# The first down-projection of a two-FFN transformer layer, rewritten as seven block products for latents and context together

## The chip, the cores and the metric

One core of one Trainium2 chip runs the whole layer as a single program. The metric is device time in microseconds (us), shorter being better. Three executions of the kernel before took 2646.32, 2648.31 and 2648.55 us, median 2648.31. A further execution was profiled and took 2648.12 us; its trace covers 2646.3 us from the first to the last instruction.

## What is computed

The layer takes 1024 latent tokens and 256 context tokens, each 1024 wide. It runs a SwiGLU feed-forward block (FFN 1), an attention stage that reads latents and context, and a second SwiGLU block (FFN 2) on the latents alone. Only FFN 1 and the modulation around it matter here:

```python
def _swiglu(h, w1, w3, w2):
    return (jax.nn.silu(h @ w1) * (h @ w3)) @ w2
...
m  = jnp.split((jax.nn.silu(c) @ w_ada[l] + b_ada[l])[:, None, :], N_MOD, axis=-1)
mc = jnp.split(jax.nn.silu(c_ctx) @ w_ada[l] + b_ada[l], N_MOD, axis=-1)
x     = _residual(x, _swiglu(_modnorm(x, g[0], m[0], m[1]), ffn1_w1[l], ffn1_w3[l], ffn1_w2[l]), g[1], m[2], HALF_STEP)
h_ctx = _residual(h_ctx, _swiglu(_modnorm(h_ctx, g[0], mc[0], mc[1]), ffn1_w1[l], ffn1_w3[l], ffn1_w2[l]), g[1], mc[2], HALF_STEP)
```

The widths are 1024 in, 2816 in the middle (22 blocks of 128), 1024 out. Everything is float32.

## The kernel before, in words

**Precision.** Every float32 operand is split into a high and a low part: ScalarE (ACT) rounds the value into the high part, VectorE (DVE) subtracts to get the low part (`split_to`, L197). A product is then three TensorE (PE) matmuls, high by high, high by low and low by high (`mm3`, L158). Every matrix that PE reads therefore costs one ACT instruction and one DVE instruction per 512 columns before it can be used.

**Order.** A stage is a `Plan` (L163): a list of main steps, each a piece of PE work, and side steps (loads, splits, sums) hung on step numbers with `spread`. The program is written out in that order, and with `pinned` set every engine executes its instructions exactly in it. Engines do not wait for a step number; they run ahead until an instruction needs something that isn't there. `store` (L134) puts a transfer to DRAM two steps later than the data is made. All transfers go through one queue, SP's.

**Stages around the change.** First comes the latents' up-projection, computed as seven block products instead of eight (Winograd's variant of Strassen's scheme; `Unit`, L458): first `plan_leads`, then `plan_rest` (L600), where the last 22 units are finished. Each latent result (silu(w1) times w3, in DRAM tensor `gd`) is stored. Then follows the down-projection. Its 22 blocks of the middle width are taken in ten groups, nine of two and one of four (`gs`, L1089). In each group every one of ten token tiles (0 to 7 latent, 8 and 9 context; 128 tokens each) does two halves of 512 output columns (`Down.tile`, L897). The result of a group is added to the sum in SBUF by DVE.

The context's up-projection is folded into these groups: 44 blocks (`ctx_up`, L1107), each 24 matmuls with 256 columns, stand between the tiles of the first nine groups (L1140). Their weights (512 KB a block) are loaded and split by side steps, and so are two parts of the modulation (`ada_steps((4, 3))`, L1168). A third part, `ada_steps((2,))`, runs beside the latents' up-projection (L1084).

In the last group the tiles finish one after the other in the order 8, 9, 0 to 7. Behind each runs a chain (`residual_steps`, L639, placed by `plan_chains`, L665): ACT squares and sums the row, POOL takes the inverse root, DVE scales and adds the residual in two instructions, ACT and POOL do the same once more, and ACT writes the normalised tile.

**The stage behind.** The projections (`punits`, L1235) use tokens 0 to 511 first: `fill0` turns tiles 0 to 3 into operand planes, and `plan_leads` then does pairs of units, each with two pieces of 12 matmuls, a first product into a PSUM bank of the pool `m` (three banks) and a second one added into the same bank. `fill1` does the same for tiles 4 to 7 while the leads run. `Unit.split` has to prepare the first four weight pieces before the leads begin (L1248).

**A model in the same kernel.** The second FFN's down-projection is already done in seven block products (`Down7`, L752): 7 products of 11 steps, each step four token tiles with three matmuls of 512 columns each, going round four PSUM banks. Its inputs are the quarter matrices (`Quarters`, L672) and the weights' differences (`WeightQuarters`, L712), which are formed during the up-projection's `plan_rest` and pass through DRAM.

Of the kernel before, what the change touches and what calls it, by code (L numbers as in the profile page):

```python
# [9 lines left out]
F32R = mybir.dt.float32r  # L10
# [5 lines left out]
P = 128  # L16
# [27 lines left out]
def hybrid_block(ctx: ExitStack, tc: tile.TileContext, a: dict, out: bass.AP):  # L44
# [234 lines left out]
    class AdaSum(Ada):  # L279


        def __init__(self, m):
            self.m = m
            self.acc = [[T2() for _ in range(2)] for _ in range(2 if m < 5 else 1)]
# [14 lines left out]
        def end(self, v, h):  # L299

            pb, s = PB("v"), ST(4)
# [7 lines left out]
    def ada_steps(ms):  # L309
# [4 lines left out]
        def step(m, k, h):  # L314
            if m not in cur:
                cur[m] = AdaSum(m)
            if k:
                cur[m].step(k - 1, h)
            if k < KD:
                cur[m].load(k, h)  # L320

        def end(m, v, h, last):
            cur[m].end(v, h)
# [428 lines left out]
    class Down7:  # L752
# [22 lines left out]
        def product(self, i, t):  # L775
# [3 lines left out]
            mm3(self.banks[t], [x[:, t * P:(t + 1) * P] for x in a], w, k == 0 and o in (0, 2, 3), k == NP - 1)  # L779
            open_group[0] = False  # L780

# [56 lines left out]
    def up_units(h, w1, w3, gd, quarters=None):  # L838
# [3 lines left out]
        def pair_(p):  # L842
# [6 lines left out]
            def emit3(i, ci, x, bank):  # L849
                y = s.pop((i, ci))  # L850
                vec.tensor_tensor(y, x, y, op=ALU.mult)
                if quarters:
                    quarters.take(p, i, ci, y)
                else:
                    store(gd[2 * p + i, :, ci * 512:(ci + 1) * 512], y)
# [8 lines left out]
    lap = [0]  # L864

    def PD():
        lap[0] = (lap[0] + 1) % 8
        return PB("smvsmvsm"[lap[0]])

    class Down:  # L870


        def __init__(self, w2, gd, ys, fs):
            self.w2, self.gd, self.ys, self.fs = w2, gd, ys, fs
            self.w, self.g, self.c, self.r = {}, {}, {}, {}

        def loads(self, f, key="v"):
            self.r[f] = load(self.w2[f], key=key), load(self.gd[f], key=key)

        def steps(self, fs=None, key="v"):  # L880

            fs = fs or self.fs

            def one(f, e):
                self.w.setdefault(f, []).append(split(self.r[f][0][:, e * 512:(e + 1) * 512]))

            def two(f):
                self.g[f] = split2(self.r.pop(f)[1])

            s = []  # L890
            for f, after in zip(fs, fs[1:] + [None]):
                s += [lambda f=f: one(f, 0), lambda f=f: one(f, 1), lambda f=f: two(f)]
                if after is not None:
                    s[-2] = lambda f=f, n=after: (one(f, 1), self.loads(n, key))
            return s

        def tile(self, t, es=range(2)):  # L897
            ys, fs = self.ys, self.fs
            g = self.g if t < 8 else self.c
            c = slice((t % 8) * P, (t % 8 + 1) * P)  # L900
            if fs[0] == 0 and 0 in es:
                ys[t] = V()
            for e in es:
                o = slice(e * 512, (e + 1) * 512)
                pd = PD()
                for x, f in enumerate(fs):
                    mm3(pd, [y[:, c] for y in g[f]], self.w[f][e], x == 0, x == len(fs) - 1)
                if fs[0] == 0:
                    act.copy(ys[t][:, o], pd)
                else:  # L910
                    vec.tensor_tensor(ys[t][:, o], ys[t][:, o], pd, op=ALU.add)

    def groups(sizes):
        f, made = 0, []
        for n in sizes:
            made.append(list(range(f, f + n)))
            f += n
        return made
# [16 lines left out]
    gd = DR([NF, P, NLAT])  # L935
    units1 = up_units(h1, a["f1w1"], a["f1w3"], gd)
# [101 lines left out]
    def shift_led(p):  # L1038
# [4 lines left out]
        store(gd[2 * p, :, 0:512], x)  # L1043
# [39 lines left out]
    plan_rest(plan, units1)  # L1083
    plan.spread(ada_steps((2,)), rest1 + 10, len(plan.main) - 10)  # L1084
# [4 lines left out]
    gs = groups((2,) * 9 + (4,))  # L1089
    ys = {}  # L1090
    xc = []
    hc = [None]

# [4 lines left out]
    steps = []  # L1098
    cw, cr, cg, cc = {}, {}, {}, {}

    def ctx_load(f, x):
        cr[f, x] = load(a[("f1w1", "f1w3")[x]][f], key="v")

    def ctx_split(f, x, e):
        cw.setdefault((f, x), []).append(split(cr[f, x][:, e * 512:(e + 1) * 512]))

    def ctx_up(f, x):  # L1107
        o = PB("m")[:, :NCTX]
        for k in range(KD):
            hi, lo = cw[f, x][k // 4]  # L1110
            b = slice((k % 4) * P, (k % 4 + 1) * P)
            mm3(o, [hi[:, b], lo[:, b]], hc[0].get(k), k == 0, k == KD - 1)
        if x == 0:
            t = cg[f] = T2()
            act.activation(t[:, :NCTX], o, AF.Silu)
        else:
            g = cg.pop(f)[:, :NCTX]
            vec.tensor_tensor(g, g, o, op=ALU.mult)
            t = T2(F32R)
            cc[f] = split_to(t[:, :NCTX], t[:, NCTX:], g)  # L1120

    downs = [Down(a["f1w2"], gd, ys, fs) for fs in gs]
    for d in downs:
        d.c = cc
    o = len(plan.main)
    plan.spread([lambda: downs[0].loads(0, "u")], o - 9, o - 8)
    plan.spread(downs[0].steps(key="u"), o - 7, o)
    plan.spread(first_steps((8, 9), xc), o - 4, o - 2)
    ups = [(f, x) for f in range(NF) for x in range(2)]
    ctx_at = []  # L1130
    pos = {}
    for i, d in enumerate(downs):
        last = i == len(downs) - 1
        o = len(plan.main)
        if last:
            for t in [8, 9] + list(range(8)):
                pos[t] = len(plan.main) + 1
                plan.step(*[lambda d=d, t=t, e=e: d.tile(t, (e,)) for e in range(2)])
        else:
            order = ([None] * 4 + list(range(10)) if i == len(downs) - 2 else  # L1140
                     [0, 1, 2, 3, 4, None, 5, None, 6, None, 7, None, None, 8, 9])
            for t in order:
                if t is None:
                    f, x = ups.pop(0)
                    ctx_at.append((len(plan.main), f, x))
                    plan.step(lambda f=f, x=x: ctx_up(f, x))
                else:
                    plan.step(lambda d=d, t=t: d.tile(t))
        e = len(plan.main)
        if i == 0:  # L1150
            plan.spread([lambda: normal(xc[0]), lambda: normal(xc[1]), make_hc], o - 1, o)
            plan.spread([lambda k=k: steps[k]() for k in range(KD)], o + 1, o + 5)
        if i < len(downs) - 2:
            n = downs[i + 1]
            plan.spread([lambda n=n: n.loads(n.fs[0])], o, o + 1)
            plan.spread(n.steps(), o + 3, e)
        elif not last:
            n = downs[i + 1]
            plan.spread([lambda n=n: n.loads(n.fs[0])], o - 2, o - 1)
            plan.spread(n.steps(), o, e)  # L1160
# [1044 lines left out]
```

## Time and profile before

| | |
|---|---|
| median of three executions | 2648.31 us (2646.32 to 2648.55) |
| profiled execution, its time / its span | 2648.12 / 2646.3 us |
| granted TensorE clock, mean | 0.995 |
| DVE / ACT / POOL busy | 1861.2 (70%) / 1173.0 (44%) / 229.1 us (9%) |
| LDWEIGHTS (PEld) busy | 2222.1 us (84%), overlaps the matmuls |
| data moved | 460.57 MB, mean 174 GB/s |
| latents' up-projection, `plan_rest` | 139.82 to 462.68 us |
| down-projection with the context's up-projection | 462.68 to 905.91 us |
| first lead unit of the projections starts | 906.70 us |
| FFN 2: `plan_rest` / down-projection | 2083.15 to 2423.86 / from 2423.86 us |

How to read the lines below. A timeline row gives the start in us from the span's start, the duration, the engine, the line of the kernel, the operation, output from inputs by the names of their pools (`bm`, `bs`, `bv` are PSUM banks; `xu`, `xv`, `t` SBUF tiles), the shape, and how many alike were merged. In brackets stands idle time before it and what ended that. A matmul's own duration overlaps the next one's, so the pace of PE is the distance between starts. A row of the windows view gives, for a stretch of the span, its length, then busy time and instruction count of PE, PEld, DVE, ACT and POOL, the granted PE clock, the share of time that the DMA engines were busy and what they moved. The first row of a window whose edges cut a merged group counts only the part inside.

### The profile page before, as it was taken

How to read it: one execution, taken by the hardware profiler on the slowest of the kernel's cores; microseconds unless marked ns; L12 is line 12 of the kernel's file. 1: busy time of each engine (PE TensorE's matmuls, PEld its weight loads, DVE VectorE, ACT ScalarE, POOL GpSimd, SP SyncE). 2: the span in 40 equal slices, each digit the busy share in tenths (PEclk: the TensorE clock that was granted, in tenths of full speed). 3: DMA queues.
4: the chain of work that ended last, by engine and by line, in shares of the span. 5: the costliest groups of instructions: out<-in, count | busy, mean ns of one | idle time of the engine just before them, and what ended most of it. 6: DMA issues, size and time to landing. Idle time of an engine off the chain costs nothing.

```text
span 2646.3 us, 38182 instructions
## 1 busy us (share of the span) xinstructions
PE 2596.5 (98%) x13610; PEld 2222.1 (84%) x13610; DVE 1861.2 (70%) x3525; ACT 1173.0 (44%) x2248; POOL 229.1 (9%) x380
## 2 busy tenths in 40 slices
PE   7999999999999999999999999999999999999998
PEld 5888888888888788799888999998788888888887
DVE  4778876587876676666467988886625788778557
ACT  4532223532223763331346987774246322224533
POOL 0000000000000400000102432221011000000001
PEclk9999999999999999999999999999999999999999
DMA  7444433453433564477789942214325566546755
GB/s 285 159 154 152 147 116 123 139 176 109 173 110 104 210 220 156 163 258 231 218 287 276 252 116 75 75 30 171 112 80 172 190 237 224 187 170 251 271 187 195
DMA packets 220429, 460.57 MB, mean 174 GB/s; under 512 B 25488, under 2 KB 64592, under 8 KB 220240
## 3 DMA queue, kind: packets, MB, share of 16 engines
q1 hardware_dynamic: 220240, 458.14, 52.3%
q8 instruction: 107, 1.75, 0.3%
q14 instruction: 82, 0.67, 0.1%
HBM read 338.71 MB, written 119.34 MB: 173 GB/s over the span
## 4 chain that ended last, share of the span: by engine, by line
PE 68%; issue 18%; DVE 6%; ACT 5%; DMA 2%; POOL 1%; SPq 0%; DVEq 0%; POOLq 0%; ACTq 0%
PE bs L153 31%; PE bm L153 19%; PE bv L153 15%; PE bm L156 2%; ACT xu L1832 1%; DVE t L120 1%; DVE xv L120 1%; DVE xu L1699 1%; DVE xu L120 1%; DMA w<-d 1%; ACT t L1858 1%; DVE t L1859 1%; PE bs L156 1%; ACT t L120 1%; POOL st L120 1%
## 5 line engine op out<-in xcount | busy, mean ns | idle before, releaser
L153 PE MATMUL bm<-xu,xu 128*128 128x512 f32 (+1 forms) x2271 | 551.1, 387 | 1.4 <-DVE xu L120 1.1
L153 PEld LDWEIGHTS bm<-xu,xu 128*128 128x128 f32 x2271 | 417.9, 188 | 83.2 <-DVE xu L120 1.9
L153 PE MATMUL bs<-xu,xu 128*128 128x512 f32 (+1 forms) x1875 | 460.5, 385 | 0.5 <-DVE xu L120 0.4
L120 ACT CAST xu<-t 128x512 fp32r<-128x512 f32 x402 | 238.7, 618 | 392.4 <-DVE t L120 333.3
L153 PEld LDWEIGHTS bs<-xu,xu 128*128 128x128 f32 x1875 | 346.9, 188 | 67.7 <-DVE xu L120 0.8
L120 DVE TENSOR_TENSOR xu<-t,xu 128x512 fp32r<-128x512 f32 x402 | 265.9, 687 | 143.0 <-ACT xu L120 143.0
L153 PE MATMUL bs<-xv,xu 128*128 128x512 f32 (+1 forms) x1488 | 354.1, 387 | 5.1 <-DVE t L120 5.1
L153 PEld LDWEIGHTS bs<-xv,xu 128*128 128x128 f32 x1488 | 278.2, 189 | 62.3 <-issue 7.1
L153 PE MATMUL bv<-xv,xu 128*128 128x512 f32 x1276 | 318.6, 389 | 0.0
L153 PEld LDWEIGHTS bv<-xv,xu 128*128 128x128 f32 x1276 | 239.5, 188 | 49.7
L120 POOL TENSOR_SCALAR st<-st 128x1 f32<-128x1 f32 x72 | 38.0, 528 | 2061.2 <-ACT t L120 1999.7
L153 PE MATMUL bs<-w,w 96*128 96x512 f32 (+3 forms) x832 | 207.2, 368 | 7.7 <-DVE st L1724 7.1
L120 DVE TENSOR_TENSOR xu<-xu,xu 128x512 fp32r<-128x512 f32 (+2 forms) x219 | 149.3, 688 | 77.3 <-ACT xu L120 75.1
L153 PE MATMUL bm<-t,xu 128*128 128x256 f32 (+1 forms) x1272 | 166.0, 288 | 0.6 <-ACT t L120 0.4
L153 PEld LDWEIGHTS bm<-t,xu 128*128 128x128 f32 x1272 | 160.7, 191 | 5.6 <-ACT t L120 0.8
L120 DVE TENSOR_TENSOR xu<-xv,xu 128x512 fp32r<-128x512 f32 (+2 forms) x184 | 131.5, 739 | 47.3 <-ACT xu L120 44.1
L120 DVE TENSOR_TENSOR t<-t,t 128x512 f32<-128x512 f32 (+2 forms) x222 | 142.4, 643 | 25.8 <-ACT t L120 22.8
L153 PE MATMUL bv<-t,w 128*128 128x256 f32 x896 | 152.1, 290 | 3.7 <-ACT t L1858 1.7
L153 PEld LDWEIGHTS bv<-t,w 128*128 128x128 f32 x896 | 133.5, 191 | 19.4 <-DVE t L1859 5.0
L153 PE MATMUL bv<-xu,xu 128*128 128x512 f32 x530 | 142.7, 390 | 0.0
L120 ACT CAST xu<-xu 128x512 fp32r<-128x512 f32 (+2 forms) x211 | 127.7, 617 | 29.0 <-DMA xu<-in_wc 11.8
L153 PEld LDWEIGHTS bs<-w,w 96*128 96x128 f32 (+1 forms) x832 | 124.1, 191 | 17.0 <-DVE st L1724 10.1
(194 smaller groups left out, 3590.1 us busy)
## 6 DMA issues: line engine op xcount, KB each, us to landing
d<-t SPq DMA_DIRECT2D x321, 256.0 KB, 2.4
t<-d SPq DMA_DIRECT2D x204, 256.0 KB, 5.2
xu<-in_f1w SPq DMA_DIRECT2D x64, 512.0 KB, 3.9
xv<-in_f1w SPq DMA_DIRECT2D x64, 512.0 KB, 3.6
xu<-in_f2w SPq DMA_DIRECT2D x58, 512.0 KB, 4.5
t<-in_wada SPq DMA_DIRECT2D x112, 256.0 KB, 3.9
w<-d SPq DMA_DIRECT2D x112, 256.0 KB, 6.5
xv<-d SPq DMA_DIRECT2D x42, 512.0 KB, 5.6
```

What stands on the lines that cost most here:

```text
L120: return lambda *x, **y: pin(f(*x, **y))
L153: return pin(nc.tensor.matmul(o, s, m, start=start, stop=stop, skip_group_check=open_group[0]))
L156: return pin(nc.tensor.transpose(o, x, i))
L1699: nc.vector.tensor_scalar(dst, src, 1.0, FMIN, op0=ALU.mult, op1=ALU.max, accum_out=m)
L1832: nc.scalar.activation(x, x, AF.Exp, bias=n_[:, s:s + 1], accum_out=l[:, i:i + 1])
L1858: nc.scalar.copy(t[0], pb)
L1859: nc.vector.tensor_tensor(t[1], pb, f32(t[0]), op=ALU.subtract)
```

## The change

Three things change, all of them in FFN 1 and its surroundings.

The down-projection becomes seven block products over latents and context together. `Down7Context` inherits from `Down7`. A step now has five matmul groups of three (four latent tiles and one for the context) over five PSUM banks; per product the banks are listed in `BANKS`, and two products add into the banks of the one before. The context's tokens are cut into halves of 128, so one token tile stands for each quarter matrix. The last three of the 77 steps are done tile by tile (`tail`), which finishes latent tiles 4 to 7 and context tile 9; latent tiles 0 to 3 and context tile 8 are complete earlier.

The context's up-projection, all 44 blocks in a row, becomes a stage of its own between the latents' up-projection and the down-projection. Its results are turned into quarters (`ContextQuarters`), stored and loaded back as the latents' are. The latents' up-projection now also feeds `Quarters` and `WeightQuarters` as FFN 2 does.

The modulation parts move one stage later: `ada_steps((2,))` stands beside the context's up-projection, `(4,)` and `(3,)` beside the down-projection. The chains of tiles 0 to 3 and 8 start two steps apart, those of 4 to 7 and 9 one tail step apart; `fill0` ends three steps before the leads begin.

```diff
+    class Down7Context(Down7):
+        TAIL = 3
+        BANKS = ("mmmvv", None, "sssmm", "mvvss", "smmvv", "mmmvv", None)
...
+        def product(self, i, t):
+            if t < 4:
+                return super().product(i, t)
...
+            c = slice((k % 4) * P, (k % 4 + 1) * P)
+            mm3(self.banks[t], [x[:, c] for x in self.c[o, k // 4]], self.w[i][1], k == 0 and self.fresh(o), k == NP - 1)
...
+        def step(self, i):
+            o, k = i // NP, i % NP
+            if k == 0 and self.fresh(o):
+                self.banks = [PB(x) for x in self.BANKS[o]]
+            for t in range(5):
+                self.product(i, t)
+            if k == NP - 1:
+                for t in range(5):
+                    self.out(o, t)
...
-    plan_rest(plan, units1)
-    plan.spread(ada_steps((2,)), rest1 + 10, len(plan.main) - 10)
+    plan_rest(plan, units1, quarters1)
+    plan.spread(wq1.steps(), rest1, len(plan.main) - 8)
...
+    plan.spread([lambda t=t: xc.append(load(xin(t))) for t in (8, 9)], o - 9, o - 8)
+    plan.spread([lambda: normal(xc[0]), lambda: normal(xc[1]), make_hc], o - 7, o - 5)
+    plan.spread([lambda k=k: steps[k]() for k in range(KD)], o - 5, o - 1)
+    plan.step(*[lambda x=x: ctx_up(x) for x in range(2 * NF)])
+    for x in range(2 * NF):
+        plan.spread([lambda x=x: ctx_load(x)], o + x - 4, o + x - 3)
+        plan.spread([lambda x=x, e=e: ctx_split(x, e) for e in range(2)], o + x - 2, o + x)
+    plan_quarters(plan, quarters1, NP - 1, o)
+    plan.spread(ada_steps((2,), True), o + 1, len(plan.main) - 1)
+    down1 = Down7Context(quarters1, wq1, cq1, ys)
+    o, tail = down1.plan(plan)
...
+    plan.spread(ada_steps((4,), tag="s"), o + 2, o + 2 * NP)
+    plan.spread(ada_steps((3,), tag="s"), o + 2 * NP + 2, o + 5 * NP + 6)
+    pos = {t: o + 5 * NP + 1 + 2 * i for i, t in enumerate((0, 1, 2, 3, 8))}
+    pos.update({t: tail + i for i, t in enumerate((4, 5, 6, 7, 9))})
...
-    plan.spread([lambda k=k: fill0s()[k]() for k in range(KD)], pos[3] + 5, o + 1)
+    plan.spread([lambda k=k: fill0s()[k]() for k in range(KD)], pos[3] + 5, o - 3)
```

Two places in the order of instructions matter below. The first is ACT in the context's up-projection. Before, in the second half of the down-projection, these rows stand there; ACTIVATE is the silu of an even block, read from a PSUM bank, and CAST the high part of a split, 256 wide for a context result, 512 or 1024 wide for weights and latent results:

```order
L120 ACTIVATE t_5615<-bm_5590 128x256
L120 CAST xu_5617<-xv_5497 128x512
L120 CAST xu_5624<-xv_5566 128x512
L120 CAST xu_5645<-xv_5566 128x512
L120 CAST t_5676<-t_5615 128x256
L120 CAST xu_5679<-xv_5499 128x1024
L120 CAST xu_5683<-xv_5627 128x512
L120 CAST xu_5704<-xv_5627 128x512
L120 ACTIVATE t_5736<-bm_5711 128x256
```

Now the same engine has, from the first blocks of the new stage on (`xu_3982`, `xu_4012`, `xu_4046`, `xu_4068` and `xu_4104` are the raw weights of blocks 0 to 4, each split in two pieces):

```order
L120 CAST xu_4062<-xu_3982 128x512
L120 CAST xu_4065<-xu_4012 128x512
L120 ACTIVATE t_4096<-bm_4071 128x256
L120 CAST xu_4098<-xu_4012 128x512
L120 CAST xu_4101<-xu_4046 128x512
L120 CAST xu_4133<-xu_4046 128x512
L120 CAST xu_4136<-xu_4068 128x512
L120 ACTIVATE t_4096<-bm_4147 128x256
L120 CAST xu_4173<-xu_4068 128x512
L120 CAST xu_4176<-xu_4104 128x512
```

The second piece of an odd block's weights (`xu_4098` from `xu_4012`) is cast behind the silu of the even block before it, and nothing stands between those two blocks on PE any more.

The second place is DVE where the projections begin. Before, around the chains of latent tiles 5 (`xv_4043`) and 6 (`xv_4101`), these rows stand there; a 512-wide row that reads a bank is the end of a tile's half, SCALAR_TENSOR_TENSOR and the 1024-wide row behind it are the chain's two instructions, and `t_7856`, `t_7860` are the low parts of the first two lead units' first pieces:

```order
L120 TENSOR_TENSOR xv_4043<-xv_4043,bs_7754 128x512
L120 TENSOR_TENSOR xv_4043<-xv_4043,bm_7772 128x512
L120 SCALAR_TENSOR_TENSOR xv_4043<-xv_4043,st_7791,xv_7496 128x1024
L120 TENSOR_TENSOR xv_4043<-xv_4043,xv_7770 128x1024
L120 TENSOR_TENSOR xv_4101<-xv_4101,bv_7804 128x512
...
L120 TENSOR_TENSOR xv_4101<-xv_4101,bs_7841 128x512
L120 TENSOR_TENSOR t_7856<-xv_7768,t_7855 128x512
L120 TENSOR_TENSOR t_7860<-xv_7786,t_7859 128x512
...
L120 SCALAR_TENSOR_TENSOR xv_4101<-xv_4101,st_7883,xv_7496 128x1024
L120 TENSOR_TENSOR xv_4101<-xv_4101,xv_7839 128x1024
```

Now, with `xv_6150`, `xv_6152`, `xv_6154` for tiles 4, 5 and 6, and `t_8252`, `t_8256` for those two low parts:

```order
L120 TENSOR_TENSOR xv_6150<-xv_6150,bm_7509 128x512
L120 TENSOR_TENSOR xu_8124<-xv_8180,xu_8122 128x512
L120 SCALAR_TENSOR_TENSOR xv_6150<-xv_6150,st_8216,xv_6009 128x1024
L120 TENSOR_TENSOR xv_6150<-xv_6150,xv_8189 128x1024
L120 TENSOR_TENSOR xv_6152<-xv_6152,bm_7510 128x512
L120 SCALAR_TENSOR_TENSOR xv_6152<-xv_6152,st_8236,xv_6009 128x1024
L120 TENSOR_TENSOR xv_6152<-xv_6152,xv_8211 128x1024
L120 TENSOR_TENSOR xv_6154<-xv_6154,bm_7511 128x512
L120 TENSOR_TENSOR t_8252<-xu_8178,t_8251 128x512
L120 TENSOR_TENSOR t_8256<-xu_8201,t_8255 128x512
L120 SCALAR_TENSOR_TENSOR xv_6154<-xv_6154,st_8264,xv_6009 128x1024
L120 TENSOR_TENSOR xv_6154<-xv_6154,xv_8231 128x1024
```

The low parts now stand behind the chains of the first two tail tiles on DVE; the operand planes' rows that stood between the chains before are done ahead now (one is left, `xu_8124`), and there is one bank row per tile instead of two.

More of the change, by code (lines that the diff above doesn't have):

```diff
@@ L851, in emit3 @@
                 vec.tensor_tensor(y, x, y, op=ALU.mult)
[L852 to L855, printed above, removed]
+                quarters.take(p, i, ci, y)
             for w, emit in ((w1, emit1), (w3, emit3)):
@@ L862, in up_units @@
         return units
[L864 to L911, printed above, removed]
@@ L1092, in hybrid_block @@
     hc = [None]
+    steps = []
     def make_hc():
@@ L1096, in make_hc, with ctx_load, ctx_split @@
         steps.extend(hc[0].fill(xc, a0, mod[0]))
[L1098 to L1107, printed above, removed]
+    cw, cr = {}, {}
+    def ctx_load(x):
+        cr[x] = load(a[("f1w1", "f1w3")[x % 2]][x // 2])
+    def ctx_split(x, e):
+        cw.setdefault(x, []).append(split(cr[x][:, e * 512:(e + 1) * 512]))
@@ L1122, in hybrid_block @@
-    downs = [Down(a["f1w2"], gd, ys, fs) for fs in gs]
-    for d in downs:
-        d.c = cc
-    o = len(plan.main)
[L1126 to L1160, printed above, removed]
@@ L1267, in hybrid_block @@
     plan_leads(plan, punits, PLEAD)
[L1268 removed]
+    plan.spread([lambda k=k: fill1s()[k]() for k in range(KD)], o + 5, o + 13)
     e = len(plan.main)
[L1270 removed]
+    plan.spread(h2.sums(), o + 13, e)
     plan_first_rest(plan, punits, e - 9, e - 5, e)
```

141 lines of the change are left out of this document (100 added, 41 removed).

## The prediction

> **What bounds the kernel now.** I read the page first, then the windows view by stage, then the timelines of PE, DVE and ACT where stages meet.
>
> ```profile
> span 2646.3 us, 38182 instructions
> PE 2596.5 (98%) x13610; PEld 2222.1 (84%) x13610; DVE 1861.2 (70%) x3525; ACT 1173.0 (44%) x2248; POOL 229.1 (9%) x380
> ```
>
> ```profile
> 139.82:384.62 244.80, 244.80 (x1081) 202.77 (x1080) 196.45 (x313) 68.02 (x117) 0.00 (x0) 1.00 0.42 142
> 462.68:890.02 427.34, 426.76 (x2405) 374.22 (x2404) 303.62 (x478) 142.87 (x263) 21.32 (x26) 1.00 0.41 140
> 890.02:945.89 55.87, 50.58 (x245) 41.38 (x244) 33.91 (x50) 43.52 (x69) 11.04 (x14) 0.97 0.67 235
> 2083.15:2273.00 189.85, 189.47 (x837) 156.59 (x836) 162.69 (x262) 53.43 (x91) 0.00 (x0) 1.00 0.66 229
> 2423.86:2631.00 207.14, 207.14 (x923) 171.65 (x922) 131.16 (x208) 95.03 (x168) 6.02 (x10) 1.00 0.67 239
> ```
>
> PE is the bound, and not only on average: in the led part of the up-projection's rest (first row) it has no idle time, in the down-projection (second) 0.58 us, at the start of the projections (third) 5.29 us. The last two rows are FFN 2, where quarters and seven products exist already: 0.38 us idle in the one, none in the other. So the kernel gets faster by what PE has less to do, less what PE newly waits. Both need PE's pace:
>
> ```profile
> 384.62 2.88 PE L153 MATMUL bm<-xu,xu 128*128 128x512 f32 x12
> 387.34 0.39 PE L153 MATMUL bs<-xv,xu 128*128 128x512 f32 x1
> 496.58 5.92 PE L153 MATMUL bm<-t,xu 128*128 128x256 f32 x48
> 502.34 0.40 PE L153 MATMUL bm<-xu,t 128*128 128x512 f32 x1
> 2427.26 0.84 PE L153 MATMUL bm<-xu,xu 128*128 128x512 f32 x3
> 2427.94 0.84 PE L153 MATMUL bs<-xu,xu 128*128 128x512 f32 x3
> ```
>
> From start to start, 12 matmuls of 512 columns take 2.72 us, 0.2267 each; two context blocks take 5.76 us, 2.88 each and 0.12 per matmul of 256 columns; three matmuls and then another bank take 0.68 us, again 0.2267 each. Going round the banks costs nothing.
>
> **The products.** Before, 22 blocks x 10 tiles x 2 halves x 3 = 1320 matmuls of 512 columns; after, 77 steps x 5 x 3 = 1155. That is 165 fewer, 165 x 0.2267 = **-37.4 us**. The context's 44 blocks, the transposes and the modulation are the same in number. All 165 lie on the path, since PE doesn't idle in this stage.
>
> **The context's up-projection by itself.** PE needs a block every 2.88 us. Before, four blocks also stand in a row once:
>
> ```profile
> 803.24 11.68 PE L153 MATMUL bm<-t,xu 128*128 128x256 f32 x96
> 806.31 0.38 ACT L120 ACTIVATE t<-bm 128x256 f32<-128x256 f32 x1 [5.48 <-PE bm L153]
> 806.59 1.65 ACT L120 CAST xu<-xv 128x512 fp32r<-128x512 f32 x3
> 807.23 1.90 DVE L120 TENSOR_TENSOR xu<-xv,xu 128x512 fp32r<-128x512 f32 x3 [2.90 <-ACT xu L120]
> ```
>
> The first of the four ends at 806.12. Its silu starts 0.19 us later, the next cast 0.47 later, that cast's low part 1.11 later, and this takes about 0.69 (three merged in 1.90, 0.60 apart). So a piece cast behind a silu has its low part 1.80 us after the even block's end. In the new order that piece is the second half of the next block, which PE reaches after 12 matmuls; its low part is used first by the third matmul from there, at 14 x 0.12 = 1.68 us. PE waits some 0.17 us, with the wake-up say 0.2, once for each of 22 pairs: **+4 us**. Bounds: nothing, if the weight load for that matmul hides it, and 22 x 0.5 = 11 us, if one more DVE instruction of 0.6 stands half in the way. No gain is possible here, since blocks already run at 2.88. DVE's work for a pair of blocks is four low parts of 0.60 to 0.69, one 256-wide product, quarter sums and modulation, some 4.5 of 5.76 us. Transfers:
>
> ```profile
> xv<-in_f1w SPq DMA_DIRECT2D x64, 512.0 KB, 3.6
> ```
>
> A load is issued four blocks ahead and first cast two blocks later, so it has 5.76 us for 3.6. But 512 KB every 2.88 us is 182 GB/s, and with the modulation's weights, quarters and first down loads I estimate 260 (33 MB in 127 us), more than the 239 of the busiest row above; this is the rival below.
>
> **The up-projection's rest takes more DVE work.** Per pair of units there are four quarter sums and four weight differences, as in FFN 2 (fourth window: DVE 162.69 of 189.85, 86%). In the first window the modulation's sums leave and 72 instructions of about 0.68 come:
>
> ```profile
> L120 DVE SCALAR_TENSOR_TENSOR t<-t,sc,t 128x512 f32<-128x512 f32 x28 | 19.7, 747 | 0.0
> ```
>
> 196.45 - 19.7 + 49 = 226 of 244.8 us, 92%. DVE's rows overlap by 0.08 each when back to back, so there is some room left, and FFN 2 runs at 86% without a stall. I take **0**, at worst +5 us. A gain is excluded, as PE is never idle there. The context tiles' preparation moves into the end of this stage; its eight half tiles are held beside the quarters in the pool of 20. I take +1 us for that (0 to 3).
>
> **Where the projections begin.** Here PE waits already:
>
> ```profile
> 887.30 2.89 PE L153 MATMUL bv<-xu,xu 128*128 128x512 f32 x12
> 890.02 0.49 PE L156 MATMUL bs<-ident,xv 128*128 128x128 f32 x3
> 894.07 1.33 PE L156 MATMUL bs<-ident,xv 128*128 128x128 f32 x5 [3.56 <-ACT xv L120]
> 895.05 4.15 PE L153 MATMUL bs<-xu,xu 128*128 128x512 f32 x12
> 899.04 1.04 PE L156 MATMUL bs<-ident,xv 128*128 128x128 f32 x8
> 939.15 0.60 PE L156 MATMUL bs<-ident,xv 128*128 128x128 f32 x4
> 939.51 3.00 PE L153 MATMUL bm<-xu,xu 128*128 128x512 f32 x12
> ```
>
> From 890.02 to 945.89 there are 15 runs of 12 (15 x 2.72 = 40.8) and 64 transposes (0.36 for four, 5.8), 46.6 us of work in 55.87: **9.3 us are lost**. Besides the wait of 3.56, the 12 matmuls behind it took 3.99 instead of 2.72; the row's granted clock is 0.97.
>
> [...]
>
> The chains set those waits, and their pace can be read:
>
> ```profile
> 860.66 0.68 DVE L120 TENSOR_TENSOR xv<-xv,bv 128x512 f32<-128x512 f32 x1
> 863.54 1.28 DVE L120 SCALAR_TENSOR_TENSOR xv<-xv,st,xv 128x1024 f32<-128x1024 f32 x1 [2.19 <-POOL st L120]
> 864.86 1.23 DVE L120 TENSOR_TENSOR xv<-xv,xv 128x1024 f32<-128x1024 f32 x1
> 866.00 0.68 DVE L120 TENSOR_TENSOR xv<-xv,bs 128x512 f32<-128x512 f32 x1
> 861.44 1.06 ACT L120 ACTIVATE t<-xv 128x1024 bf16<-128x1024 f32 x1 [3.74 <-DVE xv L120]
> 862.50 1.04 ACT L120 ACTIVATE t<-xv 128x1024 bf16<-128x1024 f32 x1
> 863.54 1.14 ACT L120 ACTIVATE xv<-xv,st 128x1024 f32<-128x1024 f32 x1
> 919.25 1.28 ACT L120 ACT_TABLE_LOAD   x1
> 920.55 0.69 ACT L120 ACTIVATE t<-bm,bg 128x512 f32<-128x512 f32 x1
> ```
>
> A tile whose last bank row starts at 860.66 lets DVE go on at 866.00: 5.34 us per tile, of which DVE idles 2.19 for ACT and POOL. Before, PE spent 5.44 us on a tile's two halves, so the chains nearly kept pace. After, the tail gives a tile only 9 x 0.2267 = 2.04 us. Count from the tail's start: its five tiles end at 2.04 + 0.36 (the last transposes of `fill0`) + 4 x 2.04 = 10.56. On DVE the first chain's instructions start at 6.05 (ACT must first finish the planes' last rows, until 3.95, then 2.10 from its square to DVE), so tile 5's bank row stands at 8.51, tile 6's at 13.85, then the two low parts. The first unit's third matmul needs the first of these, done at 15.2, and could have run at 11.0: **4.2 us**. The second unit's other piece stands behind the chains of 6 and 7, done at 25.9 for a need at 23.35, three runs of 2.72 later: **2.5**. ACT then has three squares and two copies of tiles (1.05 each) and a bank copy ahead of the third unit's cast (0.6 each): from 25.3, where tile 9 is ready, this ends at 31.75, while PE is free at 28.1: **3.6**. The fourth unit needs a bank of `m` back, behind a table load (1.28) and the gate of the first unit: **2.3**. That is 12.6, and for two waits of about 4 us the slow matmuls of 895.05, 2 x 1.27 = 2.5: 15.1 us in place of 9.3, **+6 us**. Bounds: -5 (most of it hidden, since the chains of 0 to 3 and 8 are over early) to +10.
>
> **The sum.** -37.4 + 4 + 0 + 1 + 6 = -26.4; 2648.1 of the profiled execution less 26.4 is 2621.7. It differs from the median by 0.2 us, so I say **2621.5 us**. With the bounds: -37.4 - 5 = -42, 2606; -37.4 + 11 + 5 + 3 + 10 = -8, 2640, if everything is bad at once.
>
> **Rivals.**
>
> *The chains at the boundary are hidden* (17%). DVE and ACT are free early, as tiles 0 to 3 and 8 end ten steps ahead; were 0 to 5 us left of my waits, this term would be -9 to -4 instead of +6, and with 0 to 4 for the context's stage the time 2601 to 2611. Against it: the order has both chains ahead of the low parts on DVE, and they are serial.
>
> *The transfers or splits become the bound in the context's stage* (11%). If loads land at the busiest row's 239 GB/s instead of 260, the stage's 127 us become 138; with a block at 3.3 instead of 2.88 us it is 44 x 0.42 = 18 us, and the total 2636 to 2645. For it: one queue holds stores that wait on DVE. Against it: FFN 2's down-projection is at 239 GB/s without a wait.
>
> *Slower* (5%): each block of the context's stage waits for its own split. If every block, and not the odd ones' second half alone, paid the 1.11 us from a block's end to the next low part's start, that is 44 x 1.11 = 49 us: -37.4 + 49 + 6 = +18, 2666. It decides from (37.4 - 6) / 44 = 0.71 us per block on. Against it: the rows of the order show only one piece in four behind a silu, and first halves are cast a block earlier.
>
> *Going round five banks lets the clock fall* (2%). If the down-projection ran at the pace of the run at 895.05 (3.99 for 2.72), 1155 x 0.2267 x 0.47 = 123 us more, about 2734. [...] The trace disagrees for this pattern: 0.68 us for three matmuls at a granted clock of 1.00 in FFN 2.
>
> That the change doesn't do what it says can hardly be: the number of matmuls is fixed by the code.
>
> **The numbers.** The forecast has 65%, the rivals 17, 11, 5 and 2. What a measurement of this kernel can tell from no change is about 0.2%, 5.3 us, so 2643.0 to 2653.6 is the same. Of the third case some 2% lies there. Faster: 65 + 17 + 9 = 91%; the same: 2%; slower: 7%. The range 2605 to 2637 leaves out a part of the first rival, most of the second and the last two, about 18%.
>
> **What would show it.** Right: the down-projection's 77 steps at 3.40 us each with PE idle under 2 us; the context's 44 blocks in 127 to 138 us, with small waits before every second block's lower half, put down to DVE; PE waits of about 4, 2.5, 4 and 2 us when the leads start; `plan_rest` still without gaps. Wrong: steps longer than 3.40 us, waits for DMA in the context's stage, gaps in `plan_rest`, or leads that start without a wait.

## The result and the profile after

The changed kernel takes 2624.77 us, median of four executions (2623.55 to 2629.96), against 2647.73 us for the kernel before, run beside it on the same chip (2646.32 to 2648.55). The ratio is 0.9918, with a 95% interval from 0.990 to 0.9935: 0.8% faster. The profiled execution has a span of 2622.5 us, 23.8 less than before. Its page opens so:

```profile
span 2622.5 us, 38824 instructions
PE 2562.6 (98%) x13445; PEld 2189.2 (83%) x13445; DVE 1865.9 (71%) x3589; ACT 1213.5 (46%) x2325; POOL 220.8 (8%) x380
```

There are 13610 - 13445 = 165 matmuls fewer, as counted from the code, and PE is still busy for 98% of the span. Where the 23.8 us come from is read from the starts of the same PE rows in both traces:

| stretch | before | after | difference |
|---|---|---|---|
| up to the start of `plan_rest`'s led part | 139.82 | 140.03 | +0.2 |
| rest of the up-projection (to 462.68 / 464.91) | 322.86 | 324.88 | +2.0 |
| context's up-projection and down-projection, to the first lead (906.70 / 873.68) | 444.02 | 408.77 | -35.25 |
| first lead to the projections' first wait of 1.89 us (1109.71 / 1089.32) | 203.01 | 215.64 | +12.6 |
| from there past the second such wait (1129.89 / 1107.90) | 20.18 | 18.58 | -1.6 |
| all the rest (span 2646.3 / 2622.5) | 1516.4 | 1514.6 | -1.8 |

In the windows view the columns are as before: length, busy time and count of PE, PEld, DVE, ACT, POOL, granted clock, DMA share, GB/s.

```profile
139.82:464.91 325.09, 323.80 (x1435) 267.29 (x1434) 273.69 (x444) 99.48 (x176) 1.92 (x4) 1.00 0.64 222
464.91:592.00 127.09, 125.86 (x1007) 121.60 (x1006) 94.14 (x187) 50.62 (x105) 0.00 (x0) 1.00 0.75 261
592.00:862.00 270.00, 268.64 (x1251) 223.37 (x1250) 189.12 (x311) 131.49 (x228) 12.84 (x20) 1.00 0.66 220
862.00:928.00 66.00, 56.12 (x244) 45.17 (x243) 34.67 (x45) 42.18 (x68) 13.26 (x20) 0.90 0.66 231
```

Only the last row has PE idle for long: 9.9 of 66 us, at a granted clock of 0.90. That is where the projections begin.

**The rest of the up-projection** loses 2.0 us. Two waits for DVE make up 1.3 of it, one of 0.34 us at 186.79 and this one at the transposes of the context's tiles:

```profile
452.18 0.33 PE L156 MATMUL bs<-ident,xu 128*128 128x128 f32 x1 [0.95 <-DVE xu L120]
```

Otherwise DVE carries its new work (273.69 of 325.09 us) without holding PE up.

**The context's up-projection** runs from 464.91 to 600.53, 135.62 us. Four groups of transposes take 0.35 each, which leaves 134.2 for 44 blocks; at 2.88 a block it would be 126.7. So 7.5 us are lost. They don't show as idle time of PE but as waits of its weight load, here from the waits view (total, times, longest) and then from the timelines of PEld, ACT and DVE for one pair of blocks:

```profile
PEld bm L153 <- DVE xu L120: 6.0, 23, 0.5
```

```profile
500.76 5.82 PEld L153 LDWEIGHTS bm<-t,xu 128*128 128x128 f32 x48 [0.24 <-DVE xu L120]
506.81 5.81 PEld L153 LDWEIGHTS bm<-t,xu 128*128 128x128 f32 x48 [0.24 <-DVE xu L120]
505.14 0.38 ACT L120 ACTIVATE t<-bm 128x256 f32<-128x256 f32 x1 [3.60 <-PE bm L153]
505.42 2.17 ACT L120 CAST xu<-xu 128x512 fp32r<-128x512 f32 x4
506.07 1.29 DVE L120 TENSOR_TENSOR xu<-xu,xu 128x512 fp32r<-128x512 f32 x2
```

A pair takes 506.81 - 500.76 = 6.05 us instead of 5.76. The chain is the one that the prediction drew: silu at 505.14, cast behind it at 505.42, low part at 506.07, done some 0.69 later, weights loaded from 506.81 on.

**The down-projection** goes at 3.40 us a step, as counted, round five banks (603.96 - 600.53 is 3.43 for the first, which has the change of shape in it, 607.36 - 603.96 is 3.40):

```profile
600.53 2.23 PE L153 MATMUL bm<-xu,xu 128*128 128x512 f32 x9
...
603.96 2.20 PE L153 MATMUL bm<-xu,xu 128*128 128x512 f32 x9
...
607.36 2.20 PE L153 MATMUL bm<-xu,xu 128*128 128x512 f32 x9
...
681.88 0.96 PE L153 MATMUL bs<-xu,xu 128*128 128x512 f32 x3 [1.29 <-DVE st L120]
```

Its one wait, in the last row, is at the third product, which opens banks of the pool `s`: one of them is still held by the modulation's last sum, which DVE has yet to reduce.

**The projections' beginning**, from the tail's first run of 18 matmuls to the run behind the eighth group of transposes:

```profile
865.08 4.36 PE L153 MATMUL bm<-xu,xu 128*128 128x512 f32 x18
...
873.68 0.73 PE L153 MATMUL bm<-xu,t 128*128 128x512 f32 x2 [0.17 <-ACT t L120]
877.87 7.62 PE L153 MATMUL bm<-xu,t 128*128 128x512 f32 x22 [3.46 <-DVE t L120]
891.74 8.01 PE L153 MATMUL bm<-xu,t 128*128 128x512 f32 x24 [6.25 <-ACT t L120]
899.59 5.61 PE L153 MATMUL bm<-xu,xu 128*128 128x512 f32 x24
...
927.74 22.49 PE L153 MATMUL bm<-xu,xu 128*128 128x512 f32 x98
```

Between 865.08 and 927.74 lie 192 matmuls (43.5 us) and eight groups of transposes (2.9), 46.4 of work in 62.66: 16.2 us are lost, where it was 9.3 before. Two waits, 3.46 and 6.25, make up 9.7; behind each the matmuls ran slowly, 22 in about 7.5 us where 5.0 are due and 24 in 7.85 where 5.44 are, together 4.9; the granted clock was 0.67 from 877.87 to 885.60 and 0.69 from 891.74 to 899.59. PE's order is the first products of two units (2 and 22 matmuls), then the second products of the same two (24). The second wait is put down to ACT, and ACT's timeline says why:

```profile
888.00 1.06 ACT L120 ACTIVATE t<-xv 128x1024 bf16<-128x1024 f32 x1 [2.65 <-DVE xv L120]
...
889.05 1.04 ACT L120 ACTIVATE t<-xv 128x1024 bf16<-128x1024 f32 x1
...
890.09 1.13 ACT L120 ACTIVATE xv<-xv,st 128x1024 f32<-128x1024 f32 x1
891.13 0.56 ACT L120 COPY t<-bm 128x512 f32<-128x512 f32 x1
```

The last row copies the first unit's bank. PE needs that copy to go on, since the unit's second product is added into the same bank, but in ACT's order it stands behind the squares of the chains, and the square at 888.00 waits for DVE to finish the tile before.

### The profile page after: what moved, and what is told of

The parts are those of the page before. It is cut to its first block, busy times and chain, and to the rows that moved or that the text cites. A ratio compares the mean times of both kernels' runs of the same rounds, so it can differ in the third digit from the quotient of the medians.

```text
span 2622.5 us, 38824 instructions
## 1 busy us (share of the span) xinstructions
PE 2562.6 (98%) x13445; PEld 2189.2 (83%) x13445; DVE 1865.9 (71%) x3589; ACT 1213.5 (46%) x2325; POOL 220.8 (8%) x380
## 4 chain that ended last, share of the span: by engine, by line
PE 69%; issue 17%; DVE 6%; ACT 5%; DMA 2%; POOL 0%; SPq 0%; DVEq 0%; ACTq 0%; POOLq 0%
PE bs L153 26%; PE bm L153 25%; PE bv L153 14%; PE bm L156 2%; ACT xu L1852 1%; DVE t L120 1%; DVE xu L120 1%; DVE xu L1719 1%; PE bs L156 1%; DVE xv L120 1%; ACT xu L120 1%; DVE t L1879 1%; ACT t L1878 1%; ACT t L120 1%; ACT xu L1753 0%
## 5 line engine op out<-in xcount | busy, mean ns | idle before, releaser
L153 PE MATMUL bm<-xu,xu 128*128 128x512 f32 (+1 forms) x2436 | 591.8, 387 | 1.4 <-DVE xu L120 1.1
L120 ACT CAST xu<-t 128x512 fp32r<-128x512 f32 x577 | 338.0, 617 | 454.1 <-DVE t L120 304.0
L120 DVE TENSOR_TENSOR xu<-t,xu 128x512 fp32r<-128x512 f32 x577 | 374.7, 685 | 148.6 <-ACT xu L120 148.6
L153 PE MATMUL bs<-xu,xu 128*128 128x512 f32 (+2 forms) x1677 | 409.7, 384 | 1.8 <-DVE st L120 1.3
L153 PEld LDWEIGHTS bs<-xu,xu 128*128 128x128 f32 x1677 | 309.4, 188 | 61.8 <-DVE st L120 1.7
L120 DVE TENSOR_TENSOR xu<-xu,xu 128x512 fp32r<-128x512 f32 (+1 forms) x301 | 200.9, 684 | 102.8 <-ACT xu L120 102.1
L120 DVE TENSOR_TENSOR t<-t,t 128x512 f32<-128x512 f32 (+3 forms) x310 | 199.2, 645 | 7.3 <-ACT t L120 3.9
L120 ACT CAST xu<-xu 128x512 fp32r<-128x512 f32 (+1 forms) x293 | 171.5, 615 | 29.6 <-DMA xu<-in_wc 22.1
L153 PEld LDWEIGHTS bv<-xu,xu 128*128 128x128 f32 x662 | 124.3, 188 | 25.8
L120 ACT ACTIVATE t<-t 128x512 f32<-128x512 f32 (+1 forms) x82 | 49.6, 606 | 193.9 <-DVE t L120 192.6
```

What stands on the lines that cost most here:

```text
L120: return lambda *x, **y: pin(f(*x, **y))
L153: return pin(nc.tensor.matmul(o, s, m, start=start, stop=stop, skip_group_check=open_group[0]))
```

## The experiments

Each kernel below is the changed kernel with the edit shown, run beside the kernel before. The kernel before has medians from 2647.73 to 2649.64 us in the sets of runs used here, so a difference of 1 or 2 us between medians of different sets says nothing.

**The context's matmul group left out of nine steps in eleven.** Does the gain come from matmuls at PE's pace alone?

```diff
+            o, k = i // NP, i % NP
+            if 0 < k < NP - 1:
+                return
             open_group[0] = True
-            o, k = i // NP, i % NP
```

> Leaves out the context's group of nine matmuls in the three middle steps and the fourth to tenth alike, that is in steps 1 to 9 of the eleven of each of the seven products: 7 x 9 x 3 = 189 matmuls of 512 columns, most of the context's down-projection. All casts, weight loads, silus, evictions and the order stay. Theory 1 (PE is the bound in this stage and a matmul costs 0.2267 us there, so the change's gain is the number of matmuls): 189 x 0.2267 = 42.8 us less than the changed kernel's 2624.8, that is 2582, with steps of 2.72 instead of 3.40 us. Theory 2 (the weights' casts, transfers or the units' chains hold the stage as well): steps stay over 3.0 us, PE gets idle time there, and the kernel is at 2595 or above.

Measured: 2587.25 us, ratio to before 0.9765 (0.9751 to 0.978). Each step of PE's timeline is 2.72 us:

```profile
603.51 2.20 PE L153 MATMUL bm<-xu,xu 128*128 128x512 f32 x9
...
606.23 2.20 PE L153 MATMUL bm<-xu,xu 128*128 128x512 f32 x9
```

The stage is as short as theory 1 has it, without a new wait in its steps; the leads start at 832.09 instead of 873.68, 41.6 us earlier, after a wait that is 1.4 longer. So nothing but PE bounds the steps, even at four fifths of their length, and by this price the 165 matmuls that the change takes away are worth their 37.4 us. The kernel as a whole is 37.5 us faster and not 42.8. Its profile is 41.2 us ahead where the leads end and gives 6.3 of that back later: two more waits of about 0.5 at 1281 and 1283, and slow matmuls (12 in 4.41 us from 1063.90) behind waits of 1.1 to 1.9 us that the changed kernel has too.

**Both halves of a context block's weights cast two blocks ahead.**

```diff
-        plan.spread([lambda x=x, e=e: ctx_split(x, e) for e in range(2)], o + x - 2, o + x)
+        plan.spread([lambda x=x, e=e: ctx_split(x, e) for e in range(2)], o + x - 2, o + x - 1)
```

> Both halves of a context block's up weights are cast two blocks ahead, where the second half was cast one block ahead, behind the silu of the even block. Theory 1 (the 7.5 us that the context's stage lost, about 0.29 us for each of 22 pairs, are the second half's low part, which comes late because its cast stands behind a silu): the loss falls to about 1 us, the pair of blocks takes 5.76 us again, and the kernel is 5 to 7 us faster than the changed one, about 2618.5. Theory 2 (the loss is DVE's work or the transfers at 261 GB/s, and the casts' place doesn't matter): the stage keeps its 134 us or gets longer, since the cast now waits for a load that lands in 6.0 us, and the kernel is at 2624 to 2632.

Measured: 2619.30 us, ratio 0.9888 (0.9873 to 0.9903). In PE's timeline 37 blocks stand in one row without a wait, and the stage ends at 592.86:

```profile
464.12 107.02 PE L153 MATMUL bm<-t,xu 128*128 128x256 f32 x888
...
592.86 2.23 PE L153 MATMUL bm<-xu,xu 128*128 128x512 f32 x9
```

It takes 128.74 us instead of 135.62, and the kernel is 5.5 us faster than the changed one by the medians, 6.3 by the profiled spans (2616.2 against 2622.5). The lost time was the place of one cast in four.

**Half of the context's up weights loaded.** This asks whether transfers had a part in that loss.

```diff
-        cr[x] = load(a[("f1w1", "f1w3")[x % 2]][x // 2])
+        cr[x] = load(a[("f1w1", "f1w3")[x % 2]][x // 2][:, 0:512], n=512)
...
-        cw.setdefault(x, []).append(split(cr[x][:, e * 512:(e + 1) * 512]))
+        cw.setdefault(x, []).append(split(cr[x][:, 0:512]))
```

> Loads only the first 512 of 1024 columns of each context block's up weights and casts both halves from it: 256 KB less for each of 44 blocks, so half the context's up weights are left out and replaced by the other half. The instructions of PE, ACT and DVE and their order stay. Theory 1 (the context's stage loses its 7.5 us to the place of the casts): the pair of blocks still takes 6.05 us and the kernel stays within 2 us of 2624.8. Theory 2 (the transfers at 261 GB/s hold the stage, or slow the casts down): the pair falls towards 5.76 us, and the kernel is 4 to 7 us faster, 2618 to 2621.

Measured: 2625.96 us, ratio 0.9915 (0.9898 to 0.9931). The stage's window and two rows of PEld:

```profile
464.91:592.00 127.09, 125.92 (x1008) 121.86 (x1008) 94.15 (x187) 50.63 (x105) 0.00 (x0) 1.00 0.55 181
```

```profile
500.27 5.80 PEld L153 LDWEIGHTS bm<-t,xu 128*128 128x128 f32 x48 [0.24 <-DVE xu L120]
506.31 5.82 PEld L153 LDWEIGHTS bm<-t,xu 128*128 128x128 f32 x48 [0.24 <-DVE xu L120]
```

181 GB/s instead of 261, and the pair still takes 6.04 us with the same wait of 0.24. Transfers had no part in it.

**The first two units' weights split six steps earlier.** The low parts that the first lead needs no longer stand behind the chains on DVE.

```diff
-    plan.spread([lambda u=u: u.load(0) for u in punits[:2]], o - 6, o - 4)
-    plan.spread([lambda u=u, n=n: u.split(n, "t") for n in ("11", "21") for u in punits[:2]], o - 3, o)
+    plan.spread([lambda u=u: u.load(0) for u in punits[:2]], o - 12, o - 10)
+    plan.spread([lambda u=u, n=n: u.split(n, "t") for n in ("11", "21") for u in punits[:2]], o - 9, o - 6)
```

> The first two units of the projections have their weights loaded and split six steps earlier, before the tail of the down-projection, so their low parts don't stand behind the tail's chains on DVE. Theory 1 (the waits at the boundary are two in a row: the low part of the first unit, and behind it the copy of its first bank, which stands on ACT behind the squares and copies of the chains; with the first gone the second takes most of it over): the wait of 3.46 us at the first unit's low part goes, the other grows to 7 to 10 us, and the kernel is 0 to 5 us faster, 2620 to 2625. Theory 2 (as the prediction had it, the low parts are what the leads wait for): 6 us or more faster, 2619 or below.

Measured: 2625.65 us, ratio 0.9913 (0.9898 to 0.9928): no gain. PE's timeline, from the tail's first run of 18:

```profile
863.89 4.36 PE L153 MATMUL bm<-xu,xu 128*128 128x512 f32 x18
...
872.17 5.60 PE L153 MATMUL bm<-xu,t 128*128 128x512 f32 x24
890.60 7.90 PE L153 MATMUL bm<-xu,t 128*128 128x512 f32 x24 [12.83 <-ACT t L120]
898.34 5.60 PE L153 MATMUL bm<-xu,xu 128*128 128x512 f32 x24
```

The wait for DVE is gone, and all of it is found again in one wait of 12.83 us for ACT. The first products of the first two units, 24 matmuls, now run without a stop, then the first unit's bank copy keeps PE waiting until 890.60. Counted from the tail's first run, that is 26.71 us, against 26.66 in the changed kernel (891.74 - 865.08). So the low parts alone were not what the boundary hung on. With them out of the way PE waits for the bank copy behind the chains; no run moved that copy by itself.

**The last five chains two steps apart**, with the second half of the planes and the sums two steps later.

```diff
-    pos.update({t: tail + i for i, t in enumerate((4, 5, 6, 7, 9))})
+    pos.update({t: tail + 2 * i for i, t in enumerate((4, 5, 6, 7, 9))})
...
-    plan.spread([lambda k=k: fill1s()[k]() for k in range(KD)], o + 5, o + 13)
+    plan.spread([lambda k=k: fill1s()[k]() for k in range(KD)], o + 7, o + 15)
...
-    plan.spread(h2.sums(), o + 13, e)
+    plan.spread(h2.sums(), o + 15, e)
```

> The chains of the last five tiles (4, 5, 6, 7, 9) stand two steps apart instead of one, so that the leads' low parts and bank copies come between them on DVE and ACT; the second half of the planes and the sums move two steps later. Theory 1 (the boundary's loss comes from where low parts and bank copies stand in their engines' order, behind five serial chains of 5.33 us each): of the 16 us lost there 6 to 10 go, and the kernel is at 2615 to 2619. Theory 2 (the five chains themselves, 27 us in series, are what PE has to wait for, and their order against the leads doesn't matter): the wait moves to the transposes of the tiles or to the second unit's pieces and the kernel stays at 2623 to 2628.

Measured: 2624.16 us, ratio 0.9906 (0.9891 to 0.992), the same as the changed kernel, as theory 2 has it. But PE's timeline doesn't show what theory 2 says:

```profile
864.50 4.36 PE L153 MATMUL bm<-xu,xu 128*128 128x512 f32 x18
...
879.23 3.04 PE L153 MATMUL bm<-xu,t 128*128 128x512 f32 x12 [0.85 <-ACT t L120]
884.10 3.03 PE L153 MATMUL bm<-xu,t 128*128 128x512 f32 x12 [1.84 <-ACT t L120]
...
894.95 5.78 PE L153 MATMUL bm<-xu,xu 128*128 128x512 f32 x24 [2.17 <-ACT t L120]
...
923.27 24.76 PE L153 MATMUL bm<-xu,xu 128*128 128x512 f32 x108
...
957.79 4.58 PE L153 MATMUL bs<-xv,xu 128*128 128x512 f32 x12 [4.33 <-DVE t L120]
962.21 1.78 PE L153 MATMUL bv<-xv,xu 128*128 128x512 f32 x7
```

From 864.50 to 923.27 there are 24 matmuls more than in the changed kernel's stretch, 51.8 us of work in 58.77: 6.9 are lost instead of 16.2. The boundary did gain 9.3 us. A part went again at 957.79, where PE waits 4.33 us for the sums that DVE now begins two steps later; in the changed kernel that wait is 1.37 long, and the 12 matmuls behind it take 2.84 and not 4.42. That is 4.5 us, and the profile lost 3.2 more at slow matmuls behind two waits of 1.89 (below), and 1.5 behind one of 1.11 that ends at 1779.50. Neither theory had this in full: the first had the boundary right, the second the kernel's time; the next runs try whether the 9 us can be kept.

**All edits together**, with the second modulation sum ended two steps earlier against the wait at 681.88, and **the same without the early splits**.

```diff
-    plan.spread(ada_steps((4,), tag="s"), o + 2, o + 2 * NP)
+    plan.spread(ada_steps((4,), tag="s"), o + 2, o + 2 * NP - 2)
```

> Together: both halves of a context block's up weights cast two blocks ahead, the first two units' weights loaded and split six steps earlier, the last five chains two steps apart, and the second modulation sum ended two steps earlier, before the third product opens its banks. If the terms add: 5.5 for the context's stage, as measured alone, 1.3 to 1.7 for the bank wait, 6 to 12 for the boundary (its loss of 16.2 falls to 4 to 10), that is 2606 to 2612. If the chains are serial whatever stands between them, only the first two remain: 2617 to 2619.

> As the one with all four edits, but with the first two units' weights split where the changed kernel splits them. Theory 1 (once chains stand apart, the low parts come between them and early splits bring nothing): within 2 us of the one with all four. Theory 2 (a wait of 3.5 us at the first low part stays, since it stands behind the first chain at any distance, and with it a slow clock): 3 to 6 us slower than the one with all four.

Measured: 2615.78 us (0.9874, 0.9859 to 0.9888) and 2616.15 us (0.9874, 0.9858 to 0.989). The early splits bring nothing once chains stand apart. Neither sum of the first expectation fits: 5.5 and 1.3 would give 2618. The wait at 681.88 is gone in both, and in both the sums still hold PE up for 4.33 us, as in the run before; here in the one without early splits:

```profile
949.56 5.46 PE L153 MATMUL bs<-xv,xu 128*128 128x512 f32 x12 [4.33 <-DVE t L120]
954.82 2.14 PE L153 MATMUL bv<-xv,xu 128*128 128x512 f32 x7
```

**The sums begun where the changed kernel begins them**, the second half of the planes one step earlier, with all else as in the run without early splits. The lines taken away are those of that run.

```diff
-    plan.spread([lambda k=k: fill1s()[k]() for k in range(KD)], o + 7, o + 15)
+    plan.spread([lambda k=k: fill1s()[k]() for k in range(KD)], o + 6, o + 13)
...
-    plan.spread(h2.sums(), o + 15, e)
+    plan.spread(h2.sums(), o + 13, e)
```

> As the run with all edits but the early splits; the second half of the planes is filled one step earlier and the sums begin where the changed kernel begins them, so that DVE has two steps (6.4 us) more for them. Theory 1 (of the boundary's gain of 9 us when the chains stand apart, 3 to 5 were given back 80 us later, in a wait of 4.33 us for DVE's sums and the slow clock behind it): that wait falls to 1 to 2 us, and the kernel is at 2611 to 2614. Theory 2 (the sums are DVE's total work up to there, and where they begin doesn't matter): the wait stays over 4 us, or PE waits for the planes before it, and the kernel stays at 2615 to 2618.

Measured: 2608.22 us, ratio 0.9846 (0.9833 to 0.986), better than either theory. That is 16.6 us less than the changed kernel's first median and 15.4 less than the one measured in the same set of runs (2623.64, below). PE's timeline:

```profile
854.86 4.36 PE L153 MATMUL bm<-xu,xu 128*128 128x512 f32 x18
...
869.58 3.02 PE L153 MATMUL bm<-xu,t 128*128 128x512 f32 x12 [0.84 <-ACT t L120]
874.60 3.02 PE L153 MATMUL bm<-xu,t 128*128 128x512 f32 x12 [2.00 <-ACT t L120]
...
885.44 3.02 PE L153 MATMUL bm<-xu,xu 128*128 128x512 f32 x12 [2.18 <-ACT t L120]
...
908.25 30.20 PE L153 MATMUL bm<-xu,xu 128*128 128x512 f32 x132
...
945.25 3.00 PE L153 MATMUL bs<-xv,xu 128*128 128x512 f32 x12 [1.37 <-DVE t L120]
```

From 854.86 to 908.25 the same 46.4 us of work take 53.39: 7.0 lost, and the sums' wait is back at 1.37 with full pace behind it. So 9.3 us of the boundary's loss can be had, and they were what the order of ACT and DVE cost there. In the profiles the context's stage is 6.9 us shorter (128.74, as with the earlier casts), the bank's wait of 1.29 is gone and the boundary gives 9.3: 17.5, where the spans differ by 16.1 (2622.5 and 2606.4). This profile is also 1.7 us ahead where the context's stage begins (463.25 against 464.91), and it loses 3.1 further on at two slow stretches that the changed kernel's profile lacks: 1.6 behind the second wait of 1.89, and 1.5 behind a wait of 1.11 that ends at 1764.19.

**The changed kernel once more.**

> The changed kernel once more, unaltered. Of its waits at the end of the projections two last 1.88 us; behind one of them the 12 matmuls took 4.42 us in the kernel before and 2.82 in the changed one, and in other runs none, one or both were slow. Theory 1 (whether a wait this short slows the clock is chance in each execution, not a trait of the kernel): the time is again 2623 to 2627, and a profile may show none, one or two slow runs there. Theory 2 (it follows from the distance between waits in each kernel): none is slow, as in its first profile, and the boundary again shows waits of 3.46 and 6.25 us.

Measured: 2623.64 us (2622.59 to 2628.40), ratio 0.9908 (0.9895 to 0.9922). The waits at the boundary are 3.45 and 6.27 us and no matmul is slow behind the waits of 1.88 and 1.89. That doesn't separate the two theories.

## Why the prediction was right, and where it was not

The forecast of 2621.5 us was 3.3 too low, inside its range. In the profiled executions the change is -23.8 us, where -26.4 was forecast.

- **Products, -37.4: right.** The steps take 3.40 us, and taking 189 more matmuls away shortened the stage by their number times 0.2267.
- **Context's stage, +4: the mechanism right, the size off.** It is 7.5, of which casting earlier gave 6.9 back. The low part was expected at 1.80 us after the even block's end; by the rows above it was done at about 1.81 (block's end 0.19 before the silu, at 504.95; low part done 0.69 behind its start, at 506.76). What was short is the need: the prediction counted to the third matmul, 1.68 us, and took a wait of 0.17. But the wait shows at the weight load, and one of those takes 5.81 / 48 = 0.12; 0.17 + 0.12 is the 0.29 us that a pair measured too long. That the load explains it is the arithmetic's word; that the cast's place does is shown. For a wake-up the prediction had put in 0.03; the rows have 0.05, from 506.76 to the weights' start at 506.81.
- **Rest of the up-projection, 0 and +1: right within its bounds.** It is +2.0. The two small waits for DVE, 0.34 and 0.95, are 1.3 of it; the prediction had expected this stage to stay without gaps.
- **Boundary, +6: the sum right, the steps wrong.** The loss went from 9.3 to 16.2, where 15.1 had been worked out. The first wait, 4.2 predicted and 3.46 measured, is the right one. The waits of 2.5, 3.6 and 2.3 at the second, third and fourth unit didn't come; in their place stands one of 6.25 at the first unit's second piece, and 4.9 of slow matmuls where 2.5 were reckoned, about 2.4 behind each wait where 1.27 had been taken from the 12 matmuls at 895.05. The step that failed is ACT's order: the prediction counted a bank copy behind the squares of the chains only as work ahead of the third unit's cast, and passed over that PE itself waits for the first unit's copy, and earlier. That the wrong waits add up to nearly the right loss is luck.
- **Not seen: the modulation's bank.** The third product waits 1.29 us for a bank of `s`, and the forecast had no term for it. Ending the modulation's sum two steps earlier took the wait away.
- **Luck.** 1.6 us of the gain are 12 matmuls behind a wait that both profiles have: they took 4.42 us before, at a granted clock of 0.63 (1125.47 to 1130.10), and 2.82 after, at 1.00 (1105.08 to 1108.00). Of another 1.8 us after 1107.90, 1.5 are of the same kind: behind a wait of 1.11 that ends at 1804.13 the profile of before has slow rows (four matmuls of 256 columns in 1.00 us where the profile of after has 0.62; the granted clock was 0.67 from 1804.13 to 1808.00), and behind the same wait of 1.10 at 1781.80 the profile of after has none, with a clock of 1.00 up to 1786.00. Of 0.9 between 464.91 and 1089.32, 0.58 is the idle time of PE in the stage before, and a wait for the projections' sums that grew from 0.90 to 1.37 goes the other way; the rest has no cause that a row names. Together these offset most of the 6.7 us by which the terms above were too low.
- **Rivals.** Transfers did reach the estimated rate, 261 GB/s, and a load took longer to land than its 3.6 us of before:

```profile
xu<-in_f1w SPq DMA_DIRECT2D x38, 512.0 KB, 6.0
```

  yet no engine waited for one, and halving them changed nothing. The chains were not hidden: 16.2 us are lost behind them. Blocks of the context didn't each wait, but one in two, 23 waits in all. The granted clock stayed at 1.00 while PE went round five banks for 270 us.

## What to carry to other kernels

In a stage that PE bounds, price removed matmuls at their measured distance, and list apart what PE newly waits for. Where a stage ends in serial chains, go through each engine's order behind them and list everything that the next stage needs from it, bank copies as well as operands: moving the operand ahead alone brought nothing here, and spacing the chains brought 9 us at the boundary. Moving work later to make room can lose the same time further on, so follow the queue behind it to its next wait.

## What the runs showed of the hardware

Behind short waits matmuls were slow in some cases and not in others. At the end of the projections each kernel has two waits of 1.86 to 1.89 us. Behind such a wait 12 matmuls took about 2.82 us in 13 of 22 cases and about 4.42 in 9, over eleven profiles, from none to both in one profile. The second wait before, and after:

```profile
1125.47 4.58 PE L153 MATMUL bs<-xv,xu 128*128 128x512 f32 x12 [1.88 <-DVE t L120]
1129.89 1.78 PE L153 MATMUL bv<-xv,xu 128*128 128x512 f32 x7
```

```profile
1105.08 2.98 PE L153 MATMUL bs<-xv,xu 128*128 128x512 f32 x12 [1.88 <-DVE t L120]
1107.90 1.75 PE L153 MATMUL bv<-xv,xu 128*128 128x512 f32 x7
```

The waits of 3.46, 4.33, 6.25 and 12.83 us were all followed by slow matmuls, and the longest cost no more in this way (24 in 7.74 us, 2.3 lost) than the shortest of them. Shorter waits cost time in some cases too: the nine slow stretches behind 1.86 to 1.89 us lost 1.6 us each. So did a still shorter one: each kernel has a wait of 1.10 or 1.11 us that ends at 1804.13 in the kernel before and at 1781.80 in the changed one, and behind it the matmuls were slow in six of the eleven profiles, at a cost of 1.5 us in five of them and 2.5 in one. Whether that is chance in each execution or set by the distance between waits stays open: the changed kernel was profiled twice and showed none both times. Its eight executions had mean granted clocks from 0.993 to 0.996, the lowest in the two that took longest, so the time at a slow clock is not the same in each; behind which waits it fell in those two no trace shows.
